# A two-layer streaming encoder: the sample's attention as steps inside the prompt's units

## Chip, cores and metric

The kernel runs on one core of one Trainium2 chip. The metric is the time of one execution on the device in microseconds; every launch does one inference step for a prompt of 2048 tokens and a sample of 32 tokens that share the weights.

## The reference, cut to what matters

Two layers, each `x + gate * rmsnorm(mixer(rmsnorm(x) * (1 + scale) + shift))` with shift, scale and gate from a conditioning vector. Layer 0 mixes with a gated linear recurrence (projection, convolution of four taps, scan, output projection). Layer 1 is attention with forget gates, 16 heads of 64:

```python
s = jnp.einsum("bqhd,bkhd->bhqk", q, k) * FOX_SCALE
s = s + jnp.swapaxes(cq, 1, 2)[..., :, None] - jnp.swapaxes(ck, 1, 2)[..., None, :]
s = jnp.where(kpos <= qpos, s, -jnp.inf)
o = jnp.einsum("bhqk,bkhd->bqhd", jax.nn.softmax(s, axis=-1), v)
y = (o * jax.nn.silu(g)) @ w_out
```

`cq` and `ck` are running sums of the logarithms of the forget gates. The prompt attends to itself (2048 keys, causal). The sample's 32 queries attend to 512 cached keys and values and then to their own 32. Outputs are both results, the states, and the new keys, values and gates.

## The kernel before

All is in fp32. Where fp32r operands are used in matmuls, a value is split into a high part (a copy rounded by ACT, POOL or DVE: `hi_act`, `hi_pool`, `hi_dve`, L91 to L98) and a low part (DVE subtracts the high part, `lo_dve`, L100), and a product becomes three matmuls. All DMAs are issued by SP, in program order; a DMA whose buffer is not free holds up those behind it. Buffers come from pools by role (`get`, L68): "w" has 5, "raw" 3, "half" 5, "ahalf" 12, "tiny" 20 (for tiles of 32 columns), "kv" 6, and "vs" 8 that are taken in a ring. PSUM has eight banks: two "pj" for projections and output tiles, two "st" for scores, two "mx" for maxima, one "pva" and one "pvb" for the products with values.

Layer 0 runs the tokens in two halves of 1024; the 32 of the sample go with the second. `lru_in` (L404) runs twelve blocks of columns in each half; in the second half it reads its split weights back from DRAM (`wl_d`, L420), at the start of a block those of the next. The rows of the conditioning matmuls (`ada`, L227) are slipped in behind each chunk by the generator `side` (L1365).

Layer 1: `main` (L1443) is one stream: projections of both halves (`proj`, L740, with matmuls in L831 and L870), loading the output weights, then seven output tiles (`out_tiles`, L586). `attention` (L916) is the other. `merge` (L1296) takes turns between them by a price in nanoseconds of matmul columns that each yields; attention gets 1.25 times what `main` has taken.

`attention` makes a list of jobs: for each half and each pair of heads p two prompt jobs (e = 0, 1), each with two units of 512 queries; a unit has a tile for each 128 keys (4, 8, 12 or 16). In the second half two sample jobs follow each pair, of one unit with 32 queries and five tiles (4 x 128 cached keys, 32 new ones); for the last pair they stand before it. A tile's steps are `st_step` (L1074: two score matmuls L1082 and L1086 into one "st" bank, then two exponentials, rounded and full, L1088 and L1089), `lo_step` (L1092: subtraction on DVE, running sum on POOL, L1109 and L1111) and, up to two tiles later, `pv_step` (L1122: products with the values, L1134 and L1135; at the end of a unit the sums, L1139 and L1140). Between these, the loop sets up the next unit:

```python
if nu is not None and lds is None and ready(nu):
    lds, cs, tl = setup_steps(nu)
    while lds:
        lds.pop(0)()
...
n = 0
if ti >= 1 and cs:
    n = -(-len(cs) // max(1, T - (2 if u.job.sample else 3) - ti))
for i, fn in enumerate(cs[:n]):
```

So all loads of the next unit are issued at once (queries L1023, keys L983, values L984, the row with the gates' sums L975 and L976), and its steps for the row maxima (`max_steps`, L1026: a matmul L1048 and a DVE maximum L1051 for each 128 queries and 512 keys, 9 to 16 of them) are spread over the tiles of the unit that runs. At the end of a unit the steps of its division (`fin_steps`, L1144) are put on the list `side` with a tile number; `flush_side(2)` runs at most two due ones in a tile. A sample job also loads its cached keys and values (L995, L996) and splits them (`c_sample`, L998) as one of its steps.

After `merge`, the output tiles 7 and 8 to 16 run alone. In an output tile 48 matmuls (L626) fill two banks, then ACT squares (L643), and `end` scales (DVE L652), adds (POOL L653) and stores. With a `pause` the tile yields that price before `end`.

## Time and profile before

| what | value |
|---|---|
| median of three runs | 3165.12 us (3160.25 to 3165.23) |
| the profiled execution | 3170.38 us |
| its span | 3168.6 us |
| mean granted clock of TensorE | 0.948 |
| busy: TensorE, VectorE, ScalarE, GpSimd | 2955.6, 1861.4, 1459.5, 1298.6 us |
| DMA | 488.74 MB, mean 154 GB/s |

The span is the time from the first to the last instruction in the trace. PE is TensorE's matmuls, PEld its weight loads, DVE VectorE, ACT ScalarE, POOL GpSimd, SP the engine that issues DMAs. A line number is that of the kernel before. Busy time counts an instruction from start to end; matmuls overlap. The granted clock is a share of TensorE's full speed; its lower level is one half.

### The profile page before, as it was taken

What the parts mean: (1) busy time and instruction counts of PE and PEld (TensorE: products, weight loads), DVE (VectorE), ACT (ScalarE), POOL (GpSimd) and SP (SyncE); (2) the same over time, 40 slices, a digit from 0 to 9 for tenths busy, and PEclk for the clock granted to TensorE, in tenths of its full rate; (3) what the DMA queues carried; (4) which work ended last, traced back from release to release, by engine and by line L of the source; (5) the groups of instructions that cost most, each with busy time, mean ns of one, the idle gap of its engine ahead of it and who ended that gap; (6) DMA issues with size and microseconds to landing.
All of it is one profiled execution on the core that took longest, in us unless ns stands there. A gap on an engine that the chain in (4) does not pass through costs nothing. (4 is left out here: it accounts for less than half of the span.)

```text
span 3168.6 us, 45048 instructions
## 1 busy us (share of the span) xinstructions
PE 2955.6 (93%) x14900; PEld 2351.3 (74%) x14900; DVE 1861.4 (59%) x3387; ACT 1459.5 (46%) x2992; POOL 1298.6 (41%) x1301
## 2 busy tenths in 40 slices
PE   7999899998999999999998999989998999887898
PEld 3777678896678878787876788777776877665676
DVE  7788657657222456464646556657575666675622
ACT  4455555555111435353536446545564646453611
POOL 6444343313122524343435235444454545453622
PEclk9999889999999999999998899998899989887989
DMA  7545433333533475767676644535456353535233
GB/s 278 171 167 179 166 104 132 131 127 124 174 101 105 164 238 180 243 200 236 204 233 196 182 144 124 153 98 145 128 150 152 110 152 117 142 109 123 64 119 104
DMA packets 341433, 488.74 MB, mean 154 GB/s; under 512 B 79112, under 2 KB 191880, under 8 KB 341200
## 3 DMA queue, kind: packets, MB, share of 16 engines
q1 hardware_dynamic: 341200, 485.85, 50.1%
q8 instruction: 119, 1.95, 0.3%
q14 instruction: 114, 0.93, 0.1%
HBM read 307.57 MB, written 178.14 MB: 153 GB/s over the span
## 5 line engine op out<-in xcount | busy, mean ns | idle before, releaser
L1111 POOL TENSOR_TENSOR ahalf<-ahalf,ahalf 128x512 f32<-128x512 f32 (+2 forms) x528 | 577.5, 1094 | 359.8 <-ACT ahalf L1088 342.5
L870 PE MATMUL pj<-h,w 128*128 128x512 f32 (+1 forms) x2304 | 588.8, 365 | 3.7 <-DVE half L720 2.1
L101 DVE TENSOR_TENSOR ahalf<-st,ahalf 128x512 fp32r<-128x512 f32 (+3 forms) x640 | 387.6, 607 | 277.1 <-ACT st L1089 222.7
L870 PEld LDWEIGHTS pj<-h,w 128*128 128x128 f32 x2304 | 424.6, 191 | 90.7 <-issue 4.0
L1088 ACT ACTIVATE ahalf<-st 128x512 fp32r<-128x512 f32 (+3 forms) x640 | 341.0, 533 | 311.4 <-PE st L1086 276.3
L1051 DVE TENSOR_REDUCE mxs<-mx 128x1 f32<-128x512 f32 (+5 forms) x672 | 382.9, 596 | 146.4 <-PE mx L1048 98.0
L1089 ACT ACTIVATE st<-st 128x512 f32<-128x512 f32 (+4 forms) x720 | 355.1, 494 | 0.0
L1082 PE MATMUL st<-ahalf,kv 128*128 128x512 f32 (+3 forms) x640 | 256.5, 401 | 33.5 <-DVE ahalf L101 16.9
L1048 PE MATMUL mx<-kb,qm 96*128 96x512 f32 (+5 forms) x672 | 251.9, 411 | 14.8 <-DVE mxs L1051 8.8
L1134 PE MATMUL pva<-ahalf,vs 128*128 128x512 f32 (+3 forms) x640 | 243.6, 396 | 14.4 <-ACT ahalf L1088 9.0
L1086 PE MATMUL st<-ahalf,kb 96*128 96x512 f32 (+3 forms) x640 | 252.1, 401 | 4.2 <-ACT ahalf L1069 4.0
L101 DVE TENSOR_TENSOR ahalf<-ahalf,ahalf 128x512 fp32r<-128x512 f32 (+1 forms) x163 | 141.5, 870 | 172.3 <-PE st L626 97.0
L831 PE MATMUL pj<-w,h 128*128 128x256 f32 (+3 forms) x1296 | 239.5, 290 | 0.0
L1135 PE MATMUL pvb<-ahalf,vs 128*65 128x512 f32 (+3 forms) x640 | 230.6, 372 | 2.0 <-DVE od L1163 0.8
L460 PE MATMUL pj<-h,w 128*128 128x512 f32 (+1 forms) x1056 | 228.1, 367 | 0.8 <-POOL h L95 0.7
L460 PEld LDWEIGHTS pj<-h,w 128*128 128x128 f32 x1056 | 183.0, 192 | 36.0 <-POOL h L95 1.1
L831 PEld LDWEIGHTS pj<-w,h 128*128 128x128 f32 (+1 forms) x1296 | 195.0, 188 | 11.4 <-ACT half L367 0.2
L101 DVE TENSOR_TENSOR w<-raw,w 128x1024 fp32r<-128x1024 f32 (+2 forms) x61 | 83.0, 1360 | 182.7 <-issue 84.0
L870 PE MATMUL pj<-h,raw 128*128 128x272 f32 (+1 forms) x576 | 187.9, 326 | 0.0
L1082 PEld LDWEIGHTS st<-ahalf,kv 128*128 128x128 f32 x640 | 126.8, 198 | 79.2 <-DVE ahalf L101 37.4
L626 PE MATMUL pj<-h,w 128*128 128x512 f32 x576 | 164.5, 429 | 17.3 <-DVE half L652 10.7
L1048 PEld LDWEIGHTS mx<-kb,qm 96*128 96x128 f32 (+1 forms) x672 | 129.4, 199 | 64.6 <-DVE mxs L1051 38.7
(320 smaller groups left out, 5681.4 us busy)
## 6 DMA issues: line engine op xcount, KB each, us to landing
wp_d<-w SPq DMA_DIRECT2D x60, 512.0 KB
vs<-v_d SPq DMA_DIRECT2D x96, 256.0 KB
kv<-k_d SPq DMA_DIRECT2D x192, 128.0 KB
ahalf<-q_d SPq DMA_DIRECT2D x192, 128.0 KB
raw<-in_w SPq DMA_DIRECT2D x44, 512.0 KB
ahalf<-in_ada_w SPq DMA_DIRECT2D x64, 256.0 KB
v_d<-half SPq DMA_DIRECT2D x64, 256.0 KB
w<-wp_d SPq DMA_DIRECT2D x30, 512.0 KB
```

The costliest lines, as they stand in the source:

```text
L101: dve.tensor_tensor(o, i, f(h), ALU.subtract)
L460: pe.matmul(ps[:, :b - a], l, cols(r, a, b), start=i == 0, stop=i == 23)
L831: pe.matmul(ps[:m, :nw], l, r, start=c == 0, stop=c == 23)
L870: pe.matmul(ps[:, :b - a], l, cols(r, a, b), start=c == 0, stop=c == 23)
L1048: pe.matmul(ps[:sw, :kw], u.qm[0:96, s0:s0 + sw], kb, start=True, stop=not last)
L1051: dve.tensor_reduce(u.mxs[:sw, si, c:c + 1], ps[:sw, :kw], axis=AX.X, op=ALU.max)
L1082: pe.matmul(ps[:kw, c0:nq], j.ka[k0 // 512][:, kc:kc + kw], u.qa[:, c0:nq], start=True, stop=False)
L1086: pe.matmul(ps[:kw, c0:nq], j.kb[k0 // HALF][0:96, kd:kd + kw], u.qb[0:96, c0:nq], start=False, stop=True)
L1088: act.activation(ph[:kw, c0:nq], ps[:kw, c0:nq], AF.Exp, scale=0.125)
L1089: act.activation(ps[:kw, c0:nq], ps[:kw, c0:nq], AF.Exp, scale=0.125)
L1111: pool.tensor_tensor(u.acc[:kw, c0:nq], f(ph)[:kw, c0:nq], u.acc[:kw, c0:nq], ALU.add)
L1134: pe.matmul(u.pva[:, c:nq], vs[:kw, 0:128], ph[:kw, c:nq], start=ti == 0, stop=last)
```

## The change

Ten things are changed.

- The sample jobs go from the list; every job is now a prompt job.
- A new generator, `cache_parts`, splits the cached keys and values in layer 0's second half (two of its steps behind each chunk) and stores them behind the prompt's in `k_d` and `v_d`, which get 512 more places; the sample's new keys and values follow there.
- `sample_steps` gives one sample head as a list of steps with tile numbers. They go on the list `side` when the first unit of the same head's prompt job in the second half begins. The tiles are 32 columns wide; all five score tiles lie in one "st" bank, four exponentials serve them, and the sums over keys are five matmuls. Its key, value and query buffers exist once, in a pool of their own.
- Loads of a prompt job get tile numbers: in the second half block 0 at tile 0, block 2 at tile 2, block 1 at tile 10 and block 3 at tile 3 of the job's own first unit (`u.late`).
- Pools: "ahalf" 11, "vs" 6, "tiny" 10. Two-row tiles of `ada` move to "half" in layer 0 ("ab").
- An output tile in the merge yields 1500 before and 1500 behind its end, instead of 2600 before, and neither once attention has ended.
- From that point output tiles take four banks ("st" too).
- After attention's last tile each remaining product yields 3000, each remaining side step 2000; before, all ran in one go.
- The multiplier of the last norm (`load_gp`) for the sample's rows is loaded when its tile comes.
- Three branches for sample units go.

```diff
-N_H, N_W, N_RAW, N_HALF, N_AH = 32, 5, 3, 5, 12
+N_H, N_W, N_RAW, N_HALF, N_AH = 32, 5, 3, 5, 11
-N_KV, N_VS, N_OD, N_TINY, N_FG = 6, 8, 4, 20, 8
+N_KV, N_VS, N_OD, N_TINY, N_FG = 6, 6, 4, 10, 8
...
-            if pause:
+            if pause and "end" not in flags:
                 yield pause
                 end()
                 end = None
+                yield pause
...
+    def cache_parts():
+        for p in range(NP):
+            x, ab = get("raw", [128, PAST]), get("w", [128, 2, PAST], F32R)
+            a, b = ab[:, 0, :], ab[:, 1, :]
+            sp.dma_start(x, io["ckT"][p])
+            yield
+            hi_pool(a, x)
+            yield
+            lo_dve(b, x, a)
+            for n, y in enumerate((a, b)):
+                sp.dma_start(k_d[n, p, :, SEQ:SEQ + PAST], f(y))
+        for t in range(PAST // 128):
+            for c in range(4):
+                x, v2 = get("raw", [128, 4, 64]), get("w", [128, 4, 2, 64], F32R)
+                sp.dma_start(x, io["cv"][128 * t:128 * t + 128, 256 * c:256 * c + 256])
+                yield
+                hi_pool(v2[:, :, 1, :], x)
+                yield
+                lo_dve(v2[:, :, 0, :], x, v2[:, :, 1, :])
...
-            else:
-                for i in range(j.nk // HALF):
-                    lds.append(lambda i=i: ext(i, 0, slice(HALF * i, HALF * i + HALF)))
-                lds += [lambda b=b: ld(b) for b in range(j.nk // 512)]
-            return lds, cs
+            lds = [(0, lambda i=i: ext(i, slice(HALF * i, HALF * i + HALF))) for i in range(j.nk // HALF)]
+            for b, ti in ((0, 0), (1, 1)) if j.nk == HALF else ((0, 0), (2, 2), (1, 10), (3, -3)):
+                lds.append((ti, lambda b=b: ld(b)))
+            return lds
...
+            def scores():
+                v.P = ps = bst()
+                for t in range(5):
+                    kw = 128 if t < 4 else NS
+                    o = ps[:kw, NS * t:NS * t + NS]
+                    k = slice(128 * t, 128 * t + kw)
+                    pe.matmul(o, ka[:, k], v.qa, start=True, stop=False)
+                    if t == 4:
+                        pe.matmul(o, identr[:, :kw], mask_k[:, :NS], start=False, stop=False)
+                    pe.matmul(o, kb[0:96, k], v.qb[0:96, :], start=False, stop=True)
+                v.ph, v.pl = get("sp", [128, 5 * NS], F32R), get("sp", [128, 5 * NS], F32R)
+                for r, c in parts:
+                    act.activation(v.ph[r, c], ps[r, c], AF.Exp, scale=0.125)
+                    act.activation(ps[r, c], ps[r, c], AF.Exp, scale=0.125)
...
+            steps = [load_k, load_q, load_v, None, maxima, fin, None, fin2, None, scores, None, low, products, s0,
+                     d0, None, d1, None, rc, d2, None, d3] + ([ldg, None, zz] if e else [])
+            return [(i, fn) for i, fn in enumerate(steps) if fn is not None]
...
+            if u.job.half and u is u.job.first:
+                side.extend((clock[0] + 1 + d, fn) for d, fn in sample_steps(u.job.p, u.job.e))
             for ti in range(T):
                 clock[0] += 1
                 if nu is not None and lds is None and ready(nu):
                     lds, cs, tl = setup_steps(nu)
-                    while lds:
-                        lds.pop(0)()
+                for q in (lds or [], u.late):
+                    while q and q[0][0] <= ti:
+                        q.pop(0)[1]()
...
-                    n = -(-len(cs) // max(1, T - (2 if u.job.sample else 3) - ti))
+                    n = -(-len(cs) // max(1, T - 3 - ti))
...
         while pend:
             pv_pop()
-        clock[0] += 10
-        flush_side(999)
+            yield 3000.0
+        flags.add("end")
+        clock[0] += 100
+        while side:
+            flush_side(1)
+            yield 2000.0
...
                 next(mod, None)
+                if parts is not None:
+                    next(parts, None)
+                    next(parts, None)
                 yield x
...
-        yield from out_tiles(list(range(7)), NP, z2_d, x1_d, y_o, gps, bpj, w, False, 2600.0)
+        yield from out_tiles(list(range(7)), NP, z2_d, x1_d, y_o, gps, obank, w, False, 1500.0)
```

## Rows read from the trace of the kernel before

**Rows 1.** The page: span, busy shares, TensorE's clock in 40 slices.

```profile
span 3168.6 us, 45048 instructions
...
PE 2955.6 (93%) x14900; PEld 2351.3 (74%) x14900; DVE 1861.4 (59%) x3387; ACT 1459.5 (46%) x2992; POOL 1298.6 (41%) x1301
...
PEclk9999889999999999999998899998899989887989
```

**Rows 2.** Stretches without sample units: length, busy per engine (count), clock, DMA share, GB/s.

```profile
core 0: us, PE busy (x) PEld busy (x) DVE busy (x) ACT busy (x) POOL busy (x), PEclk, DMA share, GB/s
2020.00:2100.00 80.00, 77.60 (x414) 63.56 (x413) 53.41 (x100) 48.91 (x101) 43.83 (x39) 0.98 0.49 145
...
2170.00:2250.00 80.00, 77.93 (x448) 64.61 (x447) 53.62 (x103) 49.63 (x103) 45.28 (x41) 1.00 0.40 120
...
2590.00:2670.00 80.00, 77.40 (x418) 63.30 (x418) 53.63 (x101) 49.67 (x102) 43.14 (x40) 1.00 0.49 147
```

**Rows 3.** The stretches with sample units, columns as in rows 2.

```profile
1960.00:2020.00 60.00, 54.19 (x308) 43.48 (x308) 35.99 (x85) 27.94 (x81) 25.93 (x31) 0.89 0.47 136
2100.00:2170.00 70.00, 59.80 (x281) 46.09 (x280) 39.56 (x87) 28.95 (x79) 27.28 (x33) 0.80 0.55 139
2250.00:2310.00 60.00, 56.17 (x306) 44.73 (x304) 37.81 (x87) 27.46 (x79) 25.10 (x30) 0.86 0.49 138
2390.00:2450.00 60.00, 48.81 (x245) 36.34 (x245) 36.35 (x82) 24.98 (x71) 22.52 (x29) 0.89 0.61 146
2530.00:2590.00 60.00, 54.70 (x307) 43.61 (x305) 36.41 (x85) 27.52 (x80) 25.93 (x31) 0.86 0.47 134
2670.00:2730.00 60.00, 50.06 (x246) 38.02 (x244) 33.14 (x77) 22.55 (x66) 23.35 (x30) 0.83 0.58 138
2820.00:2900.00 80.00, 69.31 (x293) 50.38 (x292) 38.67 (x102) 26.78 (x98) 30.82 (x46) 0.79 0.39 90
```

**Rows 4.** The projection's matmuls (L870) in two stretches; only PE and PEld.

```profile
2100.00:2128.00 28.00, 20.38 (x93) 14.59 (x93) 1.00 0.45 102
2128.00:2160.00 32.00, 0.00 (x0) 0.00 (x0) 0.57 0.65 170
```

**Rows 5.** Timeline of PE: start, length, instruction, idle time before it and its releaser.

```profile
2131.92 0.79 PE L1082 MATMUL st<-ahalf,kv 128*128 128x512 f32 x1 [3.62 <-DMA kv<-k_d]
...
2141.42 0.76 PE L1134 MATMUL pva<-ahalf,vs 128*128 128x512 f32 x1 [1.60 <-DMA vs<-v_d]
```

**Rows 6.** Timeline of SP's queue at the second pair.

```profile
2131.33 1.73 SPq L983 DMA_DIRECT2D kv<-k_d  x3
```

**Rows 7.** The end of attention: the stretch as in rows 2, and one wait of PE.

```profile
2990.00:3050.00 60.00, 46.58 (x160) 34.89 (x159) 13.61 (x23) 11.74 (x24) 20.64 (x18) 0.80 0.27 84
...
3001.34 0.69 PE L1139 MATMUL pvb<-ahalf,one_col 128*65 128x512 f32 x1 [4.86 <-ACT ahalf L92]
```

**Rows 8.** Groups of one shape: count, busy us, mean ns, idle before and releasers.

```profile
L1086 PE MATMUL st<-ahalf,kb 96*128 96x512 f32 x448 | 185.7, 422 | 4.2 <-ACT ahalf L1069 4.0
...
L1088 ACT ACTIVATE ahalf<-st 128x512 fp32r<-128x512 f32 x448 | 267.4, 597 | 209.1 <-PE st L1086 194.1 <-POOL ahalf L1111 5.9 <-POOL od L1193 2.7
...
L101 DVE TENSOR_TENSOR ahalf<-st,ahalf 128x512 fp32r<-128x512 f32 x448 | 308.0, 688 | 244.9 <-ACT st L1089 193.4 <-issue 24.3 <-PE pvb L1135 8.2
...
L1088 ACT ACTIVATE ahalf<-st 128x128 fp32r<-128x128 f32 x64 | 17.7, 277 | 58.0 <-PE st L1086 54.1 <-POOL ahalf L1111 3.2 <-issue 0.4
```

**Rows 9.** Second score matmuls (L1086), PE and PEld, in a plain stretch.

```profile
2170.00:2250.00 80.00, 15.52 (x41) 7.75 (x41) 1.00 0.40 120
```

**Rows 10.** PE's timeline in a sample unit; durations min/median/max of that line.

```profile
2111.48 0.81 PE L1134 MATMUL pva<-tiny,vs 128*128 128x32 f32 x5
...
L1134 PE MATMUL pva<-tiny,vs x80: 177/263/391, 1971.0 to 2891.1; 128*128 128x32 f32 x64, 32*128 32x32 f32 x16
```

**Rows 11.** Layer 0's second half as in rows 2; SP's weight loads; a conversion on POOL.

```profile
440.00:740.00 300.00, 299.35 (x1843) 270.77 (x1843) 190.43 (x288) 161.07 (x237) 86.96 (x56) 1.00 0.36 123
...
471.79 1.66 SPq L420 DMA_DIRECT2D w<-wl_d  x2
...
L95 POOL TENSOR_SCALAR ahalf<-ahalf 128x512 fp32r<-128x512 f32 x48 | 46.6, 974 | 34.0 <-DVE ahalf L101 14.8 <-DVE c L506 6.0 <-DMA ahalf<-in_ada_w 5.6
```

More of the change, by code (lines that the diff above doesn't have):

```diff
@@ L297, in ada, with load_gp @@
             yield 2 * 216
-    def load_gp(layer):
-        gp = get("gp", [128, D])
-        gs = get("gp", [NS, D])
-        sp.dma_start(gp, gp_d[layer, 0:1, :].partition_broadcast(128))
-        sp.dma_start(gs, gp_d[layer, 1:2, :].partition_broadcast(NS))
-        return gp, gs
+    def load_gp(layer, sample):
+        m = NS if sample else 128
+        if layer and sample:
+            ts = [get("ahalf", [m, 512]) for _ in range(2)]
+            for n in range(2):
+                sp.dma_start(ts[n], gp_d[layer, 1:2, 512 * n:512 * n + 512].partition_broadcast(m))
+            return ts
+        t = get("gp", [m, D])
+        sp.dma_start(t, gp_d[layer, sample:sample + 1, :].partition_broadcast(m))
+        return [t[:, 512 * n:512 * n + 512] for n in range(2)]
     flags = set()
@@ L598, in load @@
             zq[i] = []
+            if t // 16 not in gps:
+                gps[1] = load_gp(1, 1)
             for k0 in range(0, kn, kz):
@@ L943, in attention @@
                 u.idx = len(units)
-                if j.sample:
-                    u.tiles = [(t, 0, t == 4) for t in range(5)]
-                else:
-                    b = q0 // 128
-                    order = [0] + list(range(max(b, 1), b + 4)) + list(range(1, b))
-                    u.tiles = [(t, max(0, 128 * (t - b)), t >= b) for t in order]
+                b = q0 // 128
+                order = [0] + list(range(max(b, 1), b + 4)) + list(range(1, b))
+                u.tiles = [(t, max(0, 128 * (t - b)), t >= b) for t in order]
                 units.append(u)
@@ L1029, in max_steps @@
             steps = []
-            sub = [(0, NS)] if j.sample else [(128 * s, 128) for s in range(4)]
+            sub = [(128 * s, 128) for s in range(4)]
             def q2():
@@ L1037, in max_steps @@
             for si, (s0, sw) in enumerate(sub):
-                if j.sample:
-                    cl = [(0, 512, False), (512, 32, True)]
-                else:
-                    end = u.q0 + s0 + 128
-                    cl = [(c, min(512, end - c), c + 512 >= end) for c in range(0, end, 512)]
+                end = u.q0 + s0 + 128
+                cl = [(c, min(512, end - c), c + 512 >= end) for c in range(0, end, 512)]
                 u.ncl = len(cl)
@@ L1148, in fin_steps @@
             nq = u.nq
-            key = (j.half, j.p, j.sample, u.q0)
-            np_ = min(nq, 128)
+            key = (j.half, j.p, u.q0)
+            np_ = 128
             nj = nq // np_
-            dd = dns_d[2 * j.p + e] if j.sample else dn_d[u.q0 // 512 % 2, 16 * j.half + 2 * j.p + e]
+            dd = dn_d[u.q0 // 512 % 2, 16 * j.half + 2 * j.p + e]
             def s0():
                 if key not in pairs:
-                    pairs[key] = [at([128, nq]) if j.sample else get("od", [128, nq]) for _ in range(2)]
+                    pairs[key] = [get("od", [128, nq]) for _ in range(2)]
                     pairs[key].append(sm([128, 8], "rc"))
@@ L1387, in hybrid_kernel @@
             run(pre)
+            parts = cache_parts() if half else None
             run(side(until(blocks, ("free", 0, half, 0))))
@@ L1397, in hybrid_kernel @@
         run(mod)
+        run(parts)
         last = ada(1, (4, 5), bpvb, bank0, ADA_LAST, lambda i: True)
@@ L1407, in hybrid_kernel @@
         run(wout)
-        gps = load_gp(0)
+        gps = {i: load_gp(0, i) for i in range(2)}
         ones_rows()
@@ L1453, in main @@
         yield from load_wout(io["w3"], NP, w)
-        gps = load_gp(1)
-        while not all(("z", 0, p, False) in flags for p in range(NP)):
+        gps = {0: load_gp(1, 0)}
+        while not all(("z", 0, p) in flags for p in range(NP)):
             yield None
-        yield from out_tiles(list(range(7)), NP, z2_d, x1_d, y_o, gps, bpj, w, False, 2600.0)
+        yield from out_tiles(list(range(7)), NP, z2_d, x1_d, y_o, gps, obank, w, False, 1500.0)
         att["w"], att["gps"] = w, gps
@@ L1462, in hybrid_kernel @@
     vss = [get("vs", [128, 4, 130], F32R) for _ in range(N_VS)]
+    smp = [second.tile(shape, F32R, name=n, tag=n, bufs=1)
+           for n, shape in (("ka_s", [128, SK]), ("kb_s", [128, SK]), ("vs_s", [128, 5, 130]), ("qm_s", [128, NS]),
+                            ("mx_s", [128, 1, 32]))]
     def pads():
[L1466 removed]
+        for t in kbs + [smp[1]]:
             pool.memset(f(t)[64:96, :], 0.0)
[L1468 removed]
+        pool.memset(f(smp[4]), 0.0)
+        pool.memset(f(smp[4])[:, :, 0:2], 1.0)
+        for t in qms + [smp[3]]:
             pool.memset(f(t)[64:96, :], 0.0)
             pool.memset(f(t)[64:66, :], 1.0)
[L1471 removed]
+        for t in vss + [smp[2]]:
             pool.memset(f(t)[:, :, 128:130], 1.0)
[L1474 to L1475 removed]
+    merge(main(), attention(kbs, qms, vss, smp, bst, bmx, bpva, bpvb), RATIO)
+    run(out_tiles([7] + list(range(8, 17)), NP, z2_d, x1_d, y_o, att["gps"], last_banks, att["w"]))
 def kernel(**inputs):
```

185 lines of the change are left out of this document (119 added, 66 removed).

## Prediction

> **What bounds the kernel now.** I read the page's busy shares first. TensorE is busy for 93% of a span of 3168.6 us, and the clock row is at 9 or 8 tenths almost all the way, except where it falls to 8 and 7 in scattered slices of the second half [rows 1]. So the question is not which engine is the bound (it is TensorE) but where TensorE loses time: by standing idle, or by running on the lower of its two clock levels, 1.2 instead of 2.4 GHz. For any stretch I take lost time as its length less (busy time x granted clock).
>
> The second view is a table of stretches of layer 1's second half that hold no sample unit [rows 2]. Lost there: 80 - 77.60 x 0.98 = 4.0, 80 - 77.93 = 2.1 and 80 - 77.40 = 2.6 us, a mean of 2.9 in 80, or 3.6%. Each of these stretches contains a change from one head to the next, so a change of head alone is cheap.
>
> The third view is the stretches that do hold the sample's units: six pairs of heads in a stretch each, and the last two pairs in one [rows 3]. Lost there: 60 - 54.19 x 0.89 = 11.8, 70 - 59.80 x 0.80 = 22.2, 11.7, 16.6, 13.0, 18.4, and 80 - 69.31 x 0.79 = 25.2 us. That is 118.9 us in 450, or 26%.
>
> Why? A look at the second pair. From 2100 to 2128 the projection still feeds TensorE with 93 matmuls; from 2128 to 2160 it feeds it none [rows 4]. The code says why: the merge of the two streams gives attention its turn by a price in matmul columns, a sample unit has five tiles of 32 columns, and in these five tiles all the maxima, loads and the maximum chain of the next prompt unit must be set up. So attention runs alone, and its waits lie open: TensorE stands 3.62 us for keys and 1.60 us for values [rows 5]. SP issues the last three of these key loads only at 2131.33, because a whole head's four blocks are asked for at once, behind what the six key buffers still hold [rows 6]. After these waits the granted clock is 0.80 on average over the stretch [rows 3].
>
> **The change, part by part.**
>
> A. The sample's units leave the order. Its 27 matmuls per head are issued as some twenty steps, at most two a tile, behind the tiles of the first prompt unit and the next one of the same head, and the maxima of the next prompt unit are spread over 12 or 16 tiles every time. The keys and values are asked for block by block, at tiles 0, 2 and 10 and at tile 3 of the next unit, when a buffer has come free. If the stretches of [rows 3] then lose what those of [rows 2] lose, 450 x 3.6% = 16 us stay of 118.9: **-103 us**. The bounds: everything goes (-119), or the change of a pair keeps two fifths of its loss (-62), since the end of a head is still there. I take -103, because the change of head in [rows 2] is the same operation without a sample unit.
>
> B. The end of attention. In 2990 to 3050, where the last sums of probabilities and the first output tiles meet, 60 - 46.58 x 0.80 = 22.7 us are lost; one wait of 4.86 us is for the last sum [rows 7]. The change puts output-tile work between the last products, uses four banks instead of two from that point, and makes 3000 ns of attention's turn out of the 2600 before an output tile's end, half of them behind it. **-15 us**, between 0 and -23; not all, since the first use of the output weights and the last reciprocals stay.
>
> C. New waits for banks. The scores of all five sample tiles lie in one of two "st" banks from step 9 to step 11, so for two prompt tiles one bank is left. A prompt tile holds its bank through its second score matmul, two exponentials and the subtraction: 0.42 + 0.60 + 0.60 + 0.69 = 2.3 us, to which the sample's own exponentials, two of 0.28 and two small ones, add up to 1.0 [rows 8]. The step between tiles is 80 / 41 = 1.95 us [rows 9]. So the first of the two tiles is late by up to 2.3 + 1.0 - 1.95 = 1.35 us, the second by 0.4; some 2 us per head with handovers, times 16 heads: **+32 us**. Below it could be 0, since the sample's eleven score matmuls themselves fill the time; above, three late tiles of 1.35 us and 0.7 us for an "mx" bank that holds the sample's output for one step make 4.7 x 16 = 75. Queued behind a waiting score matmul on TensorE is everything: the products, the maxima and the projection, in program order. I take the middle, as the 1.95 us step is nearly as long as the chain.
>
> D. More matmuls. The sums over keys were two matmuls on an accumulated tile and become five on the tiles themselves: 30 instead of 27 per head. Five matmuls of 32 columns in a row take 0.81 us, or (0.81 - 0.26) / 4 = 0.137 us for each after the first, which has the median 0.26 [rows 10]. 3 x 16 x 0.137 = **+7 us**. [...] In exchange ACT loses six of ten exponentials per head and the conversion of cached keys, POOL the four sums of probabilities, DVE three subtractions; none of these bounds the stretch, so nothing is counted.
>
> E. Layer 0. The cached keys and values are split there, in 24 parts behind the chunks of the second half: 24 loads, 32 stores, 24 conversions on POOL and 24 on DVE, while 48 loads with their conversions leave layer 1. From 440 to 740 TensorE is busy for 299.35 of 300 us, POOL for 87 and DVE for 190 [rows 11]. A POOL conversion of 128x512 took 0.97 us there, so POOL gets 8 x 0.97 + 16 x 0.5 = 16 us more, and DVE about as much, in the shade of TensorE. The DMA share is 0.36. The cover is the weights' lead: the next block's loads go out at 471.79, at the start of a block of some 26 us. **0 us**, as long as they keep this lead; what happens otherwise is the slower rival. One "ahalf" buffer less, ten "tiny" less, two "vs" less: costed at 0, since the sample's large tiles leave these pools too. Prompt loads lose two "vs" buffers, but with a block asked for only when an old one is finished.
>
> The sum: -103 - 15 + 32 + 7 + 0 = -79 us. The profiled execution took 3170.4 us (span 3168.6 and 1.8 around it), so 3091; the median of the three runs, 3165.1, is 5 below the profiled one, so **3086 us**. A measurement of this kernel tells about 0.2%, or 6 us, from no change.
>
> **The rivals.**
>
> 1. Banks cost more. The late tiles of C come at their upper end, and the end of a pair keeps part of its loss: -103 + 40 - 15 + 75 + 7 = +4 is the extreme; half way there it is 3125 to 3150. For it: only two "st" banks, and a chain of 2.3 us against a step of 1.95. Against it: the sample's scores cover about 1.3 us of it.
>
> 2. More is gained. The steady cadence of loads also shortens the ordinary changes of head (2.9 us in 80), and the bank waits hide behind the sample's own matmuls: -119 - 23 + 0 + 3 = -139, so 3026 to 3045. For it: SP's late keys in [rows 6] come from asking too early. Against it: the low loss in [rows 2] leaves little more.
>
> 3. Slower: layer 0 loses its lead. The 24 parts take a "raw" and a "w" buffer each, from the same pools as the weights of the next block. There are five "w": this block has two, the next two, and a part one; there are three "raw": a block of odd number two, and a part one. If two parts overlap by one buffer, a weight load waits on SP, and everything behind it on SP waits too, until the block ends; then TensorE waits for 2.36 MB. At the 123 GB/s of that stretch that takes 19 us, at a full DMA share (123 / 0.36 = 342 GB/s, an estimate from the same row) 6.9 [rows 11]. Parts run beside eight blocks: 55 to 154 us, 13 us a block or 104 in the middle, which gives 3190. It decides from 10 us a block on. Against it: the pools are just large enough if a part is finished before the next begins, and POOL and DVE have room for that.
>
> 4. It does not do what it says: the steps fall behind, because two a tile is also what the prompt's own steps need. A head has 28 tiles and so 56 places, some 25 for the sample and 16 for the prompt. It doesn't bind, unless a late DMA blocks TensorE at the step that needs it; then the time stays within 6 us of 3165.
>
> **How the numbers follow.** Forecast, 3045 to 3120: 0.62. Rival 1, 3120 to 3155: 0.13. Rival 2: 0.10. Rival 3: 0.09. Rival 4, no change: 0.04. The last 0.02 are sums of small gains and losses that end between 3155 and 3159. Faster therefore 0.62 + 0.13 + 0.10 + 0.02 = 0.87, same 0.04, slower 0.09. The range reaches from rival 2's lower part to rival 1's upper part, 3030 to 3150; outside are rivals 3 and 4 and the ends of 1 and 2, less than 0.2.
>
> **What would show it.** In the profile after: stretches of 80 us from 1900 to 2850 that all lose 3 to 6 us by busy x clock, no clock under 0.9 but at the end of attention, and no matmul on "kv" that waits more than 1 us for a DMA (A). Waits of a prompt's first score matmul for DVE's subtraction, about two per head, together 20 to 50 us (C). Output tiles that follow without gaps after the last attention tile (B). In layer 0 TensorE busy for 299 of 300 us, as before (E). The prediction is wrong if layer 0 shows a wait for "w" or "raw" at each block, if the half-clock stretches at the pairs stay, or if the bank waits reach 100 us.

## Result and profile after the change

The changed kernel takes **3068.58 us** (median of four runs, 3065.66 to 3072.32) against 3165.02 for the kernel before on the same chip (four runs, 3160.25 to 3165.23). The ratio is 0.9699, 95% interval 0.9683 to 0.9716. That is 96 us less; the forecast was 3086, its range 3030 to 3150. The runs below were made in four sittings, each with the kernel before beside it (medians of 3158 to 3169 us), so they are compared by their ratios to it. One thousandth of the ratio is 3.2 us.

A line number here is that of the changed kernel. Those that answer to lines of before: first score matmul L1076 (was L1082), second L1080 (L1086), sums L1133 and L1134 (L1139, L1140), POOL's running sums L1103 and L1105 (L1109, L1111), POOL's two multiplications at the end of a pair L1183 by the reciprocals and L1187 by the gate (L1189, L1193). New lines of the sample: matmuls L1248 and L1270, division DMAs L1285, L1288, L1295, L1298, POOL L1306 and L1307.

The page of the profile after (span, busy shares, TensorE's clock in 40 slices), which answers to [rows 1]:

```profile
span 3063.9 us, 44903 instructions
...
PE 2886.6 (94%) x14948; PEld 2323.5 (76%) x14948; DVE 1836.5 (60%) x3315; ACT 1440.3 (47%) x2864; POOL 1267.3 (41%) x1233
...
PEclk9999979999999989999999899999999999999999
```

TensorE is busy for 69 us less, and from 1840 us on its clock row stays at 9. Next, stretches of the second half: length, busy per engine (count), granted clock, DMA share, GB/s. First the whole stretch from 1900 to 2860 in the kernel before:

```profile
1900.00:2860.00 960.00, 885.94 (x4723) 710.90 (x4721) 616.63 (x1253) 517.58 (x1210) 482.34 (x484) 0.93 0.47 131
```

and then the same stretch after, with four of the twelve slices it was read in:

```profile
1900.00:2860.00 960.00, 916.96 (x5157) 753.31 (x5156) 645.05 (x1294) 556.61 (x1211) 498.59 (x440) 0.98 0.58 149
...
2060.00:2140.00 80.00, 74.36 (x392) 60.20 (x392) 43.51 (x88) 41.82 (x88) 36.91 (x33) 0.96 0.57 148
2140.00:2220.00 80.00, 78.53 (x440) 64.06 (x440) 60.95 (x124) 45.94 (x100) 39.99 (x35) 1.00 0.62 157
...
2300.00:2380.00 80.00, 79.15 (x439) 65.41 (x438) 51.55 (x105) 51.22 (x110) 43.38 (x40) 1.00 0.64 153
...
2700.00:2780.00 80.00, 73.10 (x382) 59.27 (x380) 60.37 (x111) 46.42 (x96) 42.91 (x38) 0.94 0.65 161
```

Lost time (length less busy x clock) was 960 - 885.94 x 0.93 = 136 us and is 960 - 916.96 x 0.98 = 61. The twelve slices lose 0.9 to 11.3 us each, 58 in all: good ones are as good as [rows 2], and the bad ones, but for the worst, are those in which a pair of heads ends. The lowest clock of a slice is 0.94, where [rows 3] went down to 0.79. In the worst slice, 2700 to 2780, no pair ends: TensorE waits there for a subtraction on DVE that stands behind two for the output weights ("h" from "raw"):

```profile
2749.21 2.76 DVE L101 TENSOR_TENSOR h<-raw,h 128x512 fp32r<-128x512 f32 x2 [1.03 <-POOL h L95]
...
2752.64 0.58 PE L1076 MATMUL st<-ahalf,kv 128*128 128x256 f32 x1 [4.00 <-DVE ahalf L101]
```

The place was bad before as well. This stretch of the kernel before holds no sample unit and isn't among [rows 2]; it lost 90 - 80.46 x 0.92 = 16 us:

```profile
2730.00:2820.00 90.00, 80.46 (x404) 64.19 (x405) 70.40 (x123) 55.88 (x112) 52.92 (x48) 0.92 0.45 130
```

In layer 0, however, something was lost; the row that answers to the first of [rows 11]:

```profile
440.00:740.00 300.00, 289.30 (x1765) 261.12 (x1764) 198.15 (x289) 148.90 (x221) 93.23 (x74) 0.99 0.47 156
```

TensorE was busy for 299.35 of these 300 us before, and 10 us less now. The last matmul of layer 0's input projection starts at 763.9 us (746.9 before), the layer's last output-tile matmul at 1083.9 (1072.6).

What is left of waiting shows in the list of waits from 1850 to 2880 (who waited for what: us in total, times, longest), three lines of it:

```profile
POOL od L1183 <- DMA od<-dn_d: 22.3, 7, 15.1
DVE ahalf L101 <- POOL od L1187: 36.3, 9, 6.6
PE st L1076 <- DVE ahalf L101: 28.7, 18, 4.2
```

Together they make a chain at the end of each of the first seven pairs: seven of DVE's nine waits last 3.2 to 6.6 us, and the seven waits of TensorE right behind them are 20.9 of its 28.7 us. The other eleven waits of TensorE, 7.8 us, are not of this chain. One of its places, as the timeline of the three engines has it (start, length, instruction, idle time before it and its releaser):

```profile
2249.00 0.25 POOL L1306 TENSOR_TENSOR tiny<-tiny,tiny 128x32 f32<-128x32 f32 x1 [2.49 <-DVE ahalf L101]
...
2251.95 1.27 POOL L1183 TENSOR_TENSOR od<-od,od 128x512 f32<-128x512 f32 x1 [2.37 <-DMA od<-dn_d]
...
2254.40 1.26 POOL L1187 TENSOR_TENSOR od<-od,ahalf 128x512 f32<-128x512 f32 x1
...
2255.70 0.69 DVE L101 TENSOR_TENSOR ahalf<-st,ahalf 128x512 fp32r<-128x512 f32 x1 [6.03 <-POOL od L1187]
```

POOL waits for the reciprocals of the prompt's division, then multiplies twice. The second multiplication reads the gate, which lies in one of the eleven "ahalf" buffers; DVE's subtraction wants that buffer for its result and stands for 6.03 us; the scores' bank isn't free until it has run, so TensorE's next first score matmul starts at 2256.44 after 3.57 us of idle time. The matmuls behind it take 0.5 to 0.63 us instead of 0.4: from 2257.0 the granted clock is 0.5, its lower level (1.2 GHz).

### The profile page after: what moved, and what is told of

It is laid out like the page before. It is cut to its first block, busy times and chain, and to the rows that moved or that the text cites. A ratio compares the mean times of both kernels' runs of the same rounds, so it can differ in the third digit from the quotient of the medians.

```text
span 3063.9 us, 44903 instructions
## 1 busy us (share of the span) xinstructions
PE 2886.6 (94%) x14948; PEld 2323.5 (76%) x14948; DVE 1836.5 (60%) x3315; ACT 1440.3 (47%) x2864; POOL 1267.3 (41%) x1233
## 3 DMA queue, kind: packets, MB, share of 16 engines
q8 instruction: 119, 1.95, 0.3%
## 4 chain that ended last, share of the span: by engine, by line
PE 65%; DVE 9%; issue 8%; DMA 7%; POOL 5%; ACT 4%; SPq 1%; POOLq 0%; DVEq 0%; ACTq 0%
PE pj L902 15%; PE pj L465 6%; PE st L465 6%; PE pj L633 5%; PE pj L862 5%; PE st L633 4%; PE mx L1042 4%; PE st L1076 3%; PE st L1080 3%; PE pva L1128 3%; PE pvb L1129 3%; DVE ahalf L101 2%; POOL ahalf L1105 1%; DMA dn_d<-rc 1%; DVE mxs L1045 1%
## 5 line engine op out<-in xcount | busy, mean ns | idle before, releaser
L1105 POOL TENSOR_TENSOR ahalf<-ahalf,ahalf 128x512 f32<-128x512 f32 (+2 forms) x528 | 575.9, 1091 | 372.0 <-ACT ahalf L1082 358.7
L1082 ACT ACTIVATE ahalf<-st 128x512 fp32r<-128x512 f32 (+3 forms) x640 | 341.2, 533 | 359.9 <-PE st L1080 270.3
L1045 DVE TENSOR_REDUCE mxs<-mx 128x1 f32<-128x512 f32 (+3 forms) x640 | 373.3, 604 | 130.5 <-PE mx L1042 87.6
L1083 ACT ACTIVATE st<-st 128x512 f32<-128x512 f32 (+3 forms) x640 | 339.9, 531 | 0.0
L1076 PE MATMUL st<-ahalf,kv 128*128 128x512 f32 (+3 forms) x640 | 247.1, 387 | 36.9 <-DVE ahalf L101 33.8
L1080 PE MATMUL st<-ahalf,kb 96*128 96x512 f32 (+3 forms) x640 | 243.9, 388 | 1.3 <-ACT ahalf L1063 1.1
L1042 PE MATMUL mx<-kb,qm 96*128 96x512 f32 (+3 forms) x640 | 228.0, 387 | 10.6 <-DMA qm<-q_d 4.2
L101 DVE TENSOR_TENSOR ahalf<-ahalf,ahalf 128x512 fp32r<-128x512 f32 (+1 forms) x163 | 131.2, 807 | 177.4 <-ACT ahalf L92 125.5
L101 DVE TENSOR_TENSOR w<-raw,w 128x1024 fp32r<-128x1024 f32 (+3 forms) x85 | 109.0, 1282 | 194.1 <-ACT w L92 74.6
L95 POOL TENSOR_SCALAR w<-raw 128x1024 fp32r<-128x1024 f32 (+3 forms) x68 | 78.9, 1160 | 262.0 <-PE pj L902 51.2
L1076 PEld LDWEIGHTS st<-ahalf,kv 128*128 128x128 f32 x640 | 122.1, 191 | 77.1 <-DVE ahalf L101 51.4
L465 PE MATMUL st<-h,wg 128*128 128x512 f32 (+1 forms) x792 | 175.9, 377 | 1.3 <-DVE wg L101 1.3
```

The costliest lines, as they stand in the source:

```text
L101: dve.tensor_tensor(o, i, f(h), ALU.subtract)
L465: pe.matmul(ps[:, :b - a], l, cols(r, a, b), start=i == 0, stop=i == 23)
L1042: pe.matmul(ps[:sw, :kw], u.qm[0:96, s0:s0 + sw], kb, start=True, stop=not last)
L1045: dve.tensor_reduce(u.mxs[:sw, si, c:c + 1], ps[:sw, :kw], axis=AX.X, op=ALU.max)
L1076: pe.matmul(ps[:kw, c0:nq], j.ka[k0 // 512][:, kc:kc + kw], u.qa[:, c0:nq], start=True, stop=False)
L1080: pe.matmul(ps[:kw, c0:nq], j.kb[k0 // HALF][0:96, kd:kd + kw], u.qb[0:96, c0:nq], start=False, stop=True)
```

## Experiments

### What the sample's units cost, before and after

Three kernels: the kernel before without the sample's attention, the same with the loads of the prompt's keys and values staged by tile as in the change, and the changed kernel without the sample's attention.

```diff
 # kernel before: no sample jobs in the list; the gate is stored as the sample's z
-                if half:
-                    at_ = len(jobs) - (2 if p == NP - 1 else 0)
...
 # changed kernel
-            steps = [load_k, load_q, load_v, None, maxima, fin, ..., d3] + ([ldg, None, zz] if e else [])
+            steps = [None] * 22 + ([ldg, None, st] if e else [])
```

> The kernel before without the sample's attention: its sixteen units are left out, and the sample's rows of the attention output are its gate alone. Theory (the units' place in the order cost 103 us, and their 27 matmuls a head at 0.137 us cost another 59): 165 us under the kernel before, 2990 to 3015, and the stretches at the pairs lose no more than the plain ones. Rival (the change of a pair itself costs, with the new head's maxima and keys): half of the 103 stays, 3040 to 3070.

> The same, and the prompt's keys and values are asked for block by block as in the change. Theory: without sample units there is enough to do while the keys come, so this is within 5 us of the run without staging. Rival (keys asked for at once hold up SP at every change of head): 15 to 30 us under it.

> The changed kernel without the sample's steps (left out as in the run before; the cached keys are still split in layer 0). Theory: the steps cost their own 30 matmuls a head, 66 us in all, and 5 to 15 us of waits for banks: 2985 to 3000. Rival (the waits for banks are those of the prediction, 32 us or more): 2960 to 2975. Rival (the steps fill idle places of TensorE): 3020 or more.

Measured: 2978.40 us, ratio 0.9416 (0.9398 to 0.9434); 2978.65, 0.9417 (0.9399 to 0.9435); 2976.86, 0.9414 (0.9395 to 0.9432). So the sample's attention cost 3165.0 - 2978.4 = 187 us in the old order and costs 3068.6 - 2976.9 = 92 in the new one: **95 of the 96 us are there**. Without sample units staging the loads is worth nothing, so four blocks asked for at once do no harm where a unit has 12 or 16 tiles. That the late keys of [rows 5] came from a whole head's set-up in five tiles alone is argued: staging with the sample units in place wasn't tried. And without the sample the two kernels are equal, so everything else in the change adds up to about nothing. The first and the third kernel are faster than their theories had it; the third lies just above the range of its rival (waits for banks of 32 us or more), which the runs on the bank below speak against.

### The end of attention as before

```diff
-            if pause and "end" not in flags:
+            if pause:
...
-            yield 3000.0
-        flags.add("end")
-        clock[0] += 100
-        while side:
-            flush_side(1)
-            yield 2000.0
+        clock[0] += 10
+        flush_side(999)
...
-        yield from out_tiles(list(range(7)), NP, z2_d, x1_d, y_o, gps, obank, w, False, 1500.0)
+        yield from out_tiles(list(range(7)), NP, z2_d, x1_d, y_o, gps, bpj, w, False, 2600.0)
```

> The changed kernel with the end as before: 2600 before an output tile's end and nothing behind it, two banks within the merge, all last products and side steps in one go. Theory (term B, 15 predicted and 21 read from the two traces from the last score matmul on): 3083 to 3092. Rival (the end is shorter because fewer attention tiles are left when the projections are done): within 6 us of the changed kernel, 3063 to 3075.

Measured: 3074.37 us, ratio 0.9722 (0.9702 to 0.9742), against 0.9699 of the change. The re-paced end is worth some 0.0023 x 3165 = 7 us, with intervals that overlap; that is the rival's range (3063 to 3075 us), not the theory's. The traces agree on the place: from the last score matmul to the last output matmul it takes 147.1 us in the changed kernel and 158.5 here, but here the last score matmul comes 2.8 us sooner, since output tiles leave attention more of the turns before.

### Layer 0: the parts, and the buffers of "ada"

First the cached keys and values stored unsplit, by plain copies behind layer 0 (the splitting is left out: both places get the raw values). Then a pool of its own for the conditioning rows that now share "half".

```diff
-            parts = cache_parts() if half else None
...
+        cache_plain()      # 8 + 8 tiles loaded, each stored twice
```

```diff
-        set_roles(big, "half", N_HALF, "ab")
+        set_roles(first, "ab", 3, "ab")
```

> The changed kernel without the splitting of the cached keys and values beside layer 0's blocks; they are copied unsplit to their places between the layers instead, so the sample's scores and products use wrong low parts. Theory (the parts hold up weight loads on SP; layer 0 ended 17 us later in the changed kernel): 10 to 17 us under the changed kernel, 3052 to 3059. Rival (the two-row tiles in the pool of five hold them up): within 5 us of it.

> The changed kernel; the two-row tiles of the conditioning get a pool of three of their own in layer 0 instead of sharing the five that hold the gates' weights. Theory: within 5 us of the changed kernel, since the parts cost layer 0 its 17 us. Rival (the shared five are the cause): 10 to 17 us under it.

Measured: 3070.56 us, ratio 0.9695 (0.9678 to 0.9712), and 3073.96, 0.9702 (0.9680 to 0.9724); neither differs from the change. But the first one's trace shows what the parts do (the same stretch as above, now without parts):

```profile
440.00:740.00 300.00, 296.81 (x1812) 268.06 (x1812) 191.40 (x281) 159.86 (x234) 87.89 (x56) 0.99 0.36 123
```

7.5 of the 10 lost us come back, and the input projection's last matmul starts at 752.1 instead of 763.9. The layer still ends at 1084.9, because the plain copies then run beside its output tiles, so the run can't say what the parts cost in all. In the changed kernel SP's waits from 440 to 760 name the mechanism:

```profile
SPq L692 <- DVE w L101: 39.5, 9, 5.7
...
SPq L425 <- DMA v_d<-w: 12.1, 4, 3.6
```

L692 is the store of a value part: SP stands 39.5 us in nine waits for DVE's subtraction, with the weights' loads behind it in its queue; and L425, a load of weights, waits four times until the store of a part has left its "w" buffer. Neither wait exists in the kernel before.

### The prompt's multiplications two tiles later

```diff
-                steps += [(5, ldg), (6, zz), (6, zy)]
+                steps += [(7, ldg), (8, zz), (8, zy)]
```

> The changed kernel; the two multiplications of a prompt pair's output on POOL and the load of its gate stand two tiles later (7 and 8 instead of 5 and 6). Theory (once a pair DVE's subtraction waits 4 us for a buffer that POOL frees, and POOL waits for a reciprocal's DMA; 36 us of DVE idle in 9 waits): 15 to 30 us under the changed kernel, 3040 to 3053, and no wait of DVE for that multiplication. Rival (the gate's buffer is held as long and something else waits as much): within 6 us, 3062 to 3075.

Measured: 3072.28 us, ratio 0.9701 (0.9683 to 0.9719): no gain. DVE still waits for the multiplication by the gate, 26.4 us in seven waits. POOL waits for the reciprocals in four places instead of seven, but the gate's buffer is given back no sooner, and that is what DVE waits for: from the first score matmul of the second unit of a pair's second head to the end of that multiplication it takes 26.8 us, as a median over the eight pairs, and 26.5 in the change. So the edit moved it by 0.3 us and not by two tiles.

### The bank held four tiles instead of two

```diff
-            steps = [..., scores, None, low, products, s0,
-                     d0, None, d1, None, rc, d2, None, d3] + ([ldg, None, zz] if e else [])
+            steps = [..., scores, None, None, None, low, products, s0,
+                     d0, d1, None, rc, d2, None, d3] + ([ldg, None, zz] if e else [])
```

> The changed kernel; the sample's scores keep their bank for four tiles instead of two (the subtraction two tiles later, all later steps but the last ones with it). Theory (two tiles with one bank cost little, as the sample's own matmuls fill the time): up to 12 us over the changed kernel, 3068 to 3080. Rival (term C of the prediction, 32 us for two tiles): 25 us or more over it, 3093 and up.

Measured: 3046.91 us (3044.24 to 3050.40), ratio 0.9616 (0.9596 to 0.9636). The bank is held twice as long, and the kernel is **faster** by 0.0083 x 3165 = 26 us. So a bank held longer is not what the sample still costs. From here on the question was where these 26 us come from. The waits that fell are those of the chain shown above (the same two lines of the list, in this kernel):

```profile
DVE ahalf L101 <- POOL od L1187: 21.7, 7, 4.8
PE st L1076 <- DVE ahalf L101: 17.9, 17, 3.1
```

SP's queue suggests why. First the changed kernel at the third pair (start, length, DMA; L1160, L1163, L1170, L1173 are the prompt's division, L1285 to L1298 the sample's):

```profile
2235.66 0.39 SPq L1160 DMA_DIRECT2D dn_d<-od  x1
...
2240.63 0.32 SPq L1295 DMA_DIRECT2D dns_d<-rc  x1
...
2242.22 0.32 SPq L1170 DMA_DIRECT2D dn_d<-rc  x1
...
2245.64 0.45 SPq L1298 DMA_DIRECT2D tiny<-dns_d  x1
...
2248.56 0.45 SPq L1173 DMA_DIRECT2D od<-dn_d  x1
```

and the same place with the later steps:

```profile
2225.09 0.39 SPq L1160 DMA_DIRECT2D dn_d<-od  x1
...
2231.72 0.33 SPq L1170 DMA_DIRECT2D dn_d<-rc  x1
2232.09 0.43 SPq L1295 DMA_DIRECT2D dns_d<-rc  x1
...
2234.22 0.54 SPq L1173 DMA_DIRECT2D od<-dn_d  x1
...
2237.02 0.45 SPq L1298 DMA_DIRECT2D tiny<-dns_d  x1
```

In the changed kernel the sample's store of its reciprocals (L1295) goes first. The load that needs them (L1298) goes 5.0 us later, and SP stands 2.6 of these waiting for it:

```profile
SPq L1298 <- DMA dns_d<-rc: 2.6, 1, 2.6
SPq L1173 <- DMA dn_d<-rc: 1.8, 1, 1.8
```

The prompt's load (L1173) stands behind it in the queue, and its own store (L1170), issued behind the sample's, then hasn't landed yet either: 6.3 us from that store to that load. With the later steps the prompt's store goes first and takes 2.5. From the first DMA of the prompt's division to the last it is 2248.56 - 2235.66 = 12.9 us in the one and 9.1 in the other. The other pairs are alike: at the end of the first unit of the second head the sample's store goes first in seven of the eight pairs of the changed kernel and in none with the later steps, and the medians over the eight are 12.8 and 9.1 us. The Trainium skill says in "DMA: Bandwidth & Descriptors", section "Anatomy of one DMA — SWDGE (gpsimd) path", that any wait for a semaphore happens on the issuing sequencer before dispatch. The section is on DMAs issued by GpSimd; here SP issues them, and the trace agrees: both waits, 2.6 and 1.8 us, are SP's.

### Order, place or buffer: three kernels that part them

The first moves the products and what follows to tile 14 but leaves the subtraction, and so the bank, as in the change. The second moves them to tile 20. The third leaves the steps and takes the gate out of "ahalf".

```diff
-            steps = [..., None, low, products, s0, d0, None, d1, None, rc, d2, None, d3] + ...
+            steps = [..., None, low] + [None] * K + [products, s0, d0, d1, None, rc, d2, None, d3] + ...   # K = 2; 8
```

```diff
                 def ldg():
-                    u.sg = at([128, nq])
-                    sp.dma_start(u.sg, sg_d[j.p, :, u.q0:u.q0 + nq])
+                    sp.dma_start(pairs[key][1], sg_d[j.p, :, u.q0:u.q0 + nq])
...
-                steps += [(5, ldg), (6, zz), (6, zy)]
+                steps += [(6, zz), (6, ldg), (8, zy)]
```

> The sample's products go from tile 12 of its head to tile 14, and the steps behind them (its division) with them; the subtraction stays at tile 11, so the "st" bank is held for two tiles as in the changed kernel. On SP the sample's and the prompt's division loads and stores then stand in the same order as in after_bank_long. Theory Q, the queue: the gain of after_bank_long is SP's order. In the changed kernel the sample's last load (it waits for its reciprocal to land, 31.2 us in 15 waits) stands ahead of the prompt's, the prompt's two multiplications on POOL come late, and DVE's subtraction waits for the gate's "ahalf" buffer. Then this run has the time of after_bank_long: ratio 0.959 to 0.964. Theory L, the subtraction: DVE's three small subtractions at tile 11 are in the way at the end of the first unit and are better two tiles later. Then nothing changes: ratio 0.968 to 0.972.

> As after_prod14, but the products at tile 20, so that the sample's division stands behind the whole of the prompt's on SP (in the second head of all pairs). Theory Q: the prompt's chain is as free as without a sample, and the waits of DVE for the multiplication with the gate fall from 26 to 36 us (changed kernel) to under 12: ratio 0.953 to 0.962. Theory U, the unit's end: what gained in after_bank_long is only that the products leave tile 12, where the unit changes; then this run is like after_bank_long, 0.959 to 0.964, with the waits of DVE for the gate as large as there (22.7 us). Theory L: 0.968 to 0.972.

> The changed kernel with its steps where they are; the prompt's gate (128x512) no longer takes an "ahalf" buffer, but is loaded into the buffer of the reciprocals once these have been multiplied in. Theory Q: the gate's buffer is the link by which a late multiplication on POOL stops DVE and so TensorE; without it the waits of DVE for that multiplication (36 us) are gone and a good part of the 53 us of TensorE's idle time in the second half with them: ratio 0.958 to 0.966. Against it, the load of the gate now waits on SP for POOL's first multiplication, and keys and values queue behind it. If the buffer isn't the link, or that new wait costs as much: 0.968 to 0.974.

Measured: products at 14, 3043.56 us, ratio 0.9639 (0.9610 to 0.9667); at 20, 3051.45, 0.9657 (0.9631 to 0.9683); gate elsewhere, 3051.27, 0.9659 (0.9633 to 0.9686). The first has the gain of the long bank, within the noise, with the bank held for two tiles. So theory L falls, and what counts is when the steps behind the subtraction run. The third shows the link: with the steps of the change as they are, but no gate in "ahalf", no wait of DVE for a multiplication by the gate is left in the list, and TensorE's waits for the subtraction fall from 28.7 to 13.0 us:

```profile
PE st L1076 <- DVE ahalf L101: 13.0, 16, 4.1
```

The second, with the sample wholly behind the prompt, was to be the best by theory Q and isn't; theory U doesn't fit it either, which expected DVE's waits for the gate to stay. Its waits:

```profile
DVE ahalf L101 <- POOL od L1187: 4.5, 7, 1.2
...
PE st L1076 <- DVE ahalf L101: 9.8, 12, 4.4
PE st L1076 <- DMA ahalf<-q_d: 7.8, 4, 2.5
```

Those for the gate are down from 36.3 to 4.5, as expected, but a new line has come: the next pair's queries are late, since SP now works on the sample's division when they are due. In the third kernel it is the sums at a unit's end that take up some of it:

```profile
PE pvb L1133 <- ACT ahalf L92: 11.2, 3, 4.1
```

### In between: products at tile 16

```diff
+            ... + [None] * 4 + [products, s0, d0, d1, ...]
```

> The sample's products at tile 16, between after_prod14 and after_prod20. On SP the prompt's first three division DMAs then stand ahead of the sample's second, and the prompt's last ahead of the sample's third. Theory Q: the prompt's chain is as free as in after_prod20 (waits of DVE for the multiplication with the gate under 10 us instead of 19.7 in after_prod14), and the sample's chain ends four tiles earlier than there, so that the next pair's query loads aren't held up on SP (there 7.8 us of TensorE's waits in four, here under 3): both losses are avoided, ratio 0.958 to 0.964. Theory U (only leaving the unit's end counts, SP's order doesn't): the waits of DVE for the gate and the time stay those of after_prod14, 0.962 to 0.966. If the chain of the sample merely moves its collision to another place each time: 0.964 to 0.968, with new waits of TensorE of 15 us or more by other releasers.

Measured: 3054.03 us (3047.13 to 3055.80), ratio 0.9651 (0.9632 to 0.9671). The wait for queries is gone as expected (0.6 us), that for the gate is 13.6 us, not under 10, and the sums wait as in the third kernel:

```profile
DVE ahalf L101 <- POOL od L1187: 13.6, 8, 5.8
PE st L1076 <- DVE ahalf L101: 12.4, 13, 4.1
PE pvb L1133 <- ACT ahalf L92: 9.1, 4, 3.3
```

So the hoped-for 0.958 to 0.964 was missed. The time is one that theory U (0.962 to 0.966) and the moved collision (0.964 to 0.968) allowed; against U as it was put stand the waits for the gate, 13.6 us where tile 14 has 19.7. One number sums up the series. From the first score matmul of the second unit of a pair's second head to the end of the multiplication by the gate it takes, as a median over the eight pairs: 26.5 us in the change; 22.5, 21.9, 22.3 and 21.8 with the long bank and the products at 14, 16 and 20; 21.8 without the sample. All four give those 4 us back, and all four gain 13 to 26 us. With the gate elsewhere it takes 28.7 us, the longest of all, and the kernel is still faster than the change, by 13 us with intervals that just touch: it is the buffer that makes lateness dear. The pool's size seems to have a part in it. Without the sample, the changed kernel with its eleven "ahalf" buffers has 17.0 us of DVE's waits for the gate's buffer in the same list, and the kernel before with its twelve has none; the change with twelve wasn't tried. Nor was SP's order changed by itself, so it is argued and not shown that the order, and not the later place of the steps, gives the rest of the 26 us. Beyond that the five can't be told apart: their intervals overlap, if barely, and each trades the wait for a smaller one at the end of the pair (TensorE's idle time from 1840 to 3000 is 54 us in the change and 40 to 45 in these).

## Why the prediction was right

The verdict and the range held (3068.6 in 3030 to 3150, faster), and the likeliest case with them (3045 to 3120). The sum was -79; it became -96 between the medians, and -105 between the two profiled executions (3170.4 and 3065.7). That the forecast is only 17 us off is in part luck, as C was put some 32 too high and B and E together 15 to 19 too low. Term by term:

**A, the sample's units, -103: right.** A, C and D together were put at -64; the pair of runs without the sample gives -95. With D at its measured 5 and C near nothing that leaves A at about -100; the waits for the gate's buffer, which the prediction didn't have, are left in it. The reading behind it also holds: the old units cost 187 us, of which the lost time that I counted is 119. The other 68 are near the 59 that the first expectation put on the units' matmuls.

**B, the end, -15: mis-sized.** 7 us in the timed runs, not clear of the noise, and 11.4 in the traces behind the last score matmul. The row that answers to [rows 7] shows TensorE busy without a gap where 22.7 us were lost,

```profile
2990.00:3050.00 60.00, 60.00 (x262) 46.83 (x261) 15.38 (x29) 10.64 (x29) 18.19 (x18) 1.00 0.36 110
```

but that stretch now lies 80 us behind the last score matmul. Right at the end of attention, one output tile still waits 2.80 us for DVE, at 2907. The prediction had also put all of the pacing's effect at the end; giving attention fewer turns earlier takes some of it back.

**C, waits for banks, +32: wrong, the step that failed.** I took the middle between 0 and 75 because the chain through a bank (2.3 us) is nearly as long as the step between tiles (1.95). The long bank refutes it, compared with the products at tile 14: their steps are the same but for the subtraction, so two more tiles with a bank less are all that parts them, and the ratios are 0.9616 and 0.9639, no loss. So the lower end was right. That the sample's own score matmuls fill the time, as its sentence had said, is the likely reason; no run parts it from others. And yet the sign that I had named for it came true: TensorE's first score matmul waits for DVE's subtraction for 28.7 us in all, in the announced 20 to 50. That was luck, the right line for another reason in the main. There are not two per head but 18 in 16 heads, up to 4.2 us long; in seven of them, 20.9 us, the subtraction is late since it has no buffer to write to, and without the gate in that pool the line is 13.0. It stood at 14.5 us in 15 waits before the change (1850 to 2980) and is 9.8 in 11 without the sample. The costing had looked at the step "one 'ahalf' buffer less: 0" and found the sample's large tiles gone from that pool. It did not ask who holds one of the eleven when a pair ends.

**D, more matmuls, +7: right, a little high.** The products of one head in the timeline of TensorE:

```profile
2229.09 1.22 PE L1270 MATMUL mx<-fg,vs_s 128*128 128x32 f32 x10
2230.24 0.56 PE L1270 MATMUL mx<-fg,one_col 128*65 128x32 f32 x5
2230.73 0.50 PE L1128 MATMUL pva<-ahalf,vs 128*128 128x512 f32 x1
```

The five sums take 2230.73 - 2230.24 = 0.49 us, 0.098 each, so three more in 16 heads are 5 us. The 0.137 us came from matmuls with 128 columns of weights; the sums have 65. By the rule of the Trainium skill ("TensorE: Matmul & The Clock Gate", "LDWEIGHTS (loading the stationary operand)"), a weight load of 65 columns takes 54 ns, so an estimate by loads alone would be 3, the term that the second rival's sum has; no run shows 3, and the row's 5 decides. All fifteen take 1.64 us, 0.109 each: 30 x 16 = 480 matmuls at that price are about 52 of the 92 us that the sample still costs (an estimate; 16 of them have 512 columns and take longer). The page of the changed kernel without the sample's attention gives the rest:

```profile
PE 2817.0 (95%) x14468; PEld 2265.9 (76%) x14468; DVE 1802.9 (61%) x3155; ACT 1420.1 (48%) x2752; POOL 1259.5 (42%) x1217
```

TensorE is busy for 2886.6 us with it, 70 more, and the spans differ by 91. So of the other 40 about 18 are busy time beyond that price, at the lower clock for a part, and 21 are idle; the best of the moved orders recovers 26.

**E, layer 0, 0: wrong by 11 us.** The layer ends 11.3 us later. The rival's mechanism is there, parts that take "w" and "raw" buffers from the weights and stores that stop SP's queue, at a tenth of the price that I gave it (104). The forecast said "0, as long as they keep this lead" and did not count that a store waits on SP for DVE's result. The runs don't settle how the 11 us divide: without the parts 7.5 of the 10 in that stretch come back, and a pool of their own for the conditioning rows brings nothing.

The terms as measured are -95 (A, C, D), -7 to -11 (B) and +11 (E), together -91 to -95; the other 1 to 5 of the 96 us aren't located. Of the rivals, the second (more is gained) was nearest in kind: it put the waits for banks at nothing. The first and the fourth fell. The third decides nothing at 11 us. The predicted signs hold for keys (no wait of TensorE for "kv" is in the list of waits) and for the clock; layer 0's 299 of 300 was missed. The slices lose 0.9 to 11.3 us instead of 3 to 6: the prediction took [rows 2] for all stretches without sample units, but the one at 2730 to 2820 lost 16 us in 90, and its place is still the worst.

## What to carry to other kernels

A short job between long ones is dear for what must be set up under its cover rather than for its own work, and dealing it out as steps takes that away. But each step also takes a place in every in-order queue that it uses: two chains of small dependent DMAs on one queue can delay each other, and it pays to see which one has a large buffer hanging on its end. When a predicted wait shows up with the predicted size, look at how many there are and what holds the releaser before taking the mechanism as shown.

## Not expected of the hardware

The sample's 32 reciprocals, a store of 0.1 KB in pieces of 4 bytes, take longer than the prompt's 512, a store of 2 KB in pieces of 16. Where SP waits for the store, the load that reads it goes 4.6 to 5.4 us behind the sample's store (medians of the changed kernel and the four moved orders) and 2.1 us behind the prompt's, at most 3.7, in layer 1's second half of the changed kernel without the sample. Where the prompt's store was issued within 3 us behind the sample's (three places in the change), its load came 5.2 to 6.3 us later; in all three it also stood behind the sample's load. So the smaller transfer is the slower one here, and it may slow the one behind it; why wasn't tried.

The order in which instructions run isn't that of the source either; whether the chip has a part in that no run shows. The source issues the sample's multiplication on POOL (tile 24) behind the prompt's (tile 20), while in the trace of the change it stands ahead of it (2249.00 and 2251.95); moving one step by two tiles reorders others on SP and POOL. So a step's tile number is a wish, and only the trace tells its place.
